# Scan inputs of an S5 layer: full-width matmuls with two turned copies, or half-width matmuls with one

## The chip, the cores and the metric

One core of one Trainium2 chip runs the whole program; the other cores are idle. The metric is device microseconds of one execution. PE is TensorE's matmul side and PEld its weight loads; DVE is VectorE, ACT ScalarE, POOL GpSimd, SP the queue that issues most transfers. Every fp32 matmul shows as two records in the trace, and so does its weight load.

## The reference, cut to what matters

Two encoder layers over 512 tokens of width 1024. Layer 0 mixes tokens with a bidirectional diagonal state-space scan, layer 1 with a short convolution; each is followed by cross-attention into 256 memory tokens and a squared-ReLU MLP. The change is in the scan of layer 0:

```python
u = (h @ w_in).reshape(bsz, seq, SSM_GROUPS, SSM_GROUP)
for r in range(N_DIR):
    a_bar = jnp.exp(lam * dt)
    b_bar = ((a_bar - 1.0) / lam)[..., None] * b
    bu = jnp.einsum('gph,lbgh->lbgp', b_bar, u_c)
    if r == 1:
        bu = jnp.flip(bu, axis=0)
    _, states = lax.associative_scan(_ssm_combine, (a_seq, bu), axis=0)
    if r == 1:
        states = jnp.flip(states, axis=0)
    y = y + jnp.einsum('ghp,lbgp->blgh', c, states).real
```

There are 64 groups of 16 channels, 64 complex states in each group, and two directions.

## The kernel before

The scan is done in chunks of T = 8 tokens, NC = 64 chunks. Partitions 0 to 63 hold the 64 states of the forward direction, partitions 64 to 127 those of the reverse direction. What a chunk adds to the state at its end (the scan input of the chunk) is a matmul over the chunk's 8 x 16 input values; 63 sequential scan steps then run over the chunks for all 64 groups and both directions at once.

The steps around the change, each named as in the code:

- `win_mm`, `u_evac` (lines 688 to 702): the in-projection on PE, scaled by DVE, stored to DRAM and loaded again as `U[i]`, with (channel, token in chunk) on the partitions and the 64 chunks along the free side.
- `sf_gen`, `sf_transpose` (lines 494 to 519): for each block `b` of 8 groups DVE makes the coefficients `sfT` with five operations (`sf_step(b)`, which also has ACT's `bb` copies), PE transposes them with `tr` banks and ACT copies them to `sf`.
- `s_mats` (lines 523 to 531): for real and imaginary part (`ri`), eight matmuls, one for each group, fill one PSUM bank `ps_s`; ACT copies the bank into `estate`, whose free layout is (chunk, part, group). The forward half, partitions 0 to 63, is copied as it is, the reverse half with the chunks turned round, since the reverse direction starts with the last chunk.
- `q_tables`, `q_ops` (lines 452 to 457 and 535 to 538): DVE makes the output coefficients `Q`, four blocks before the scan and four between its first steps.
- `scan_ops`, `scan_run` (lines 594 to 603 and 775 to 784): the 63 steps, four dependent operations on DVE each, in place in `estate`. The first one reads chunk 0 of `estate` for all groups.
- `strips`, `y_intra`, `kvp` (lines 543 to 584 and 711 to 713): beside the scan PE computes impulse responses (`w` banks), which go through DRAM and come back as `mt`, the in-chunk part of the output, and, as filler, the keys and values of the memory (`kv0_gen`, lines 629 to 656), whose weight blocks ACT's queue loads (`kv_load`).
- `p_early`, `p_copy`, `y_carry` (lines 674 to 683 and 586 to 592): the states are copied out as carried-in states, half of them when 42 steps are done, and multiplied with `Q`.

This whole phase stands under a manual schedule: each engine runs its instructions in the order of the code, so the calls of lines 721 to 865 are the order. Small tiles of 4 KB a partition come from one pool of 30 pages, which `sf`, `sfT`, `gt` and `Q` share: a tile waits until the last reader of the page's earlier tile is done. PSUM has a pool of six banks for `tr`, `ps_s`, `w`, `u` and `y`.

Of the kernel before, what the change touches and what calls it, by code (L numbers as in the profile page):

```python
# [46 lines left out]
def tile_encoder(ctx, tc, xT, xN, memT, memN, small, b_re, b_im, c_re, c_im, a_w_in, a_w_glu,  # L47
# [31 lines left out]

    # ------------------------------------------------------------------ constants  # L80
    sm = cpool.tile([P, NSM], F32, name="sm")
# [14 lines left out]

    # ------------------------------------------------------------------ weight stream
    def wblock(w, c0, k0=0):
# [71 lines left out]
    def lin_block(xs, hooks=None):  # L170
        """One 256-column block: two psum banks, accumulated over the 8 k-tiles."""
        t = next_block()
        ps = [bank([S], "lin") for _ in range(2)]
        for k in range(KT):
            if hooks and k in hooks:
                for f in hooks[k]:
                    f()
            xh, xl = xs(k)
            for m in range(2):
                mm3(ps[m], wsl(t, k, m, 0), wsl(t, k, m, 1), xh, xl, k == 0, k == KT - 1)  # L180
        return ps

    class Act2:
        """hi/lo split activation: 8 k-tiles, two per page."""

# [27 lines left out]

    # ------------------------------------------------------------------ norm helpers
    class Stats:
# [30 lines left out]

    # ================================================================== S5 phase
    man = ExitStack()
# [29 lines left out]
    def token_rstd(srcs, dst):  # L278
        """rows of tokens -> 1/rms of every token, on all partitions of dst."""
        n = len(srcs)  # L280
        ss = s5pool.tile([P, n], F32, name=nm("ss"))
        for i in range(n):
            act.activation(srcs[i], srcs[i], AF.Square, accum_out=ss[:, i:i + 1])
        act.activation(ss, ss, AF.Sqrt, scale=1.0 / D, bias=epsb)

        def rest():
            v.reciprocal(ss, ss)
            dg = page([n, P], F32, "dg")
            for i in range(n):
                act.activation(dg[:, i, :], ident, AF.Copy, scale=ss[:, i:i + 1])  # L290
            ps = fbank([n, P], "rb")
            pe.matmul(ps, lhsT=ones, rhs=dg, start=True, stop=True)
            act.copy(dst, ps.rearrange("p n q -> p (n q)"))
        return rest

    # ---- discretisation tables, [(r,p), g]
    def sm64(o):
# [29 lines left out]
    def exp_ops(o, x):  # L327
        """o = exp(x): x = n ln2 + r, polynomial in r, exponent bits from n."""
        xc, n, r, acc = t64(), t64(), t64(), t64()
        ni = t64().bitcast(I32)  # L330
        cs = [1.0 / math.factorial(k) for k in range(9)]
        ops = [lambda: ts(xc, x, 88.5, ALU.min, -87.0, ALU.max),
               lambda: ts(n, xc, 1.0 / math.log(2.0), ALU.mult, MAGIC, ALU.add),
               lambda: ts(n, n, -MAGIC, ALU.add),
               lambda: stt(r, n, -0.693359375, xc, ALU.mult, ALU.add),
               lambda: stt(r, n, 2.12194440e-4, r, ALU.mult, ALU.add),
               lambda: ts(n, n, 127.0, ALU.add, float(2**23), ALU.mult),
               lambda: ts(acc, r, cs[8], ALU.mult),
               lambda: v.tensor_copy(ni, n)]
        for k in range(7, 0, -1):  # L340
            ops.append(lambda k=k: stt(acc, acc, cs[k], r, ALU.add, ALU.mult))
        ops.append(lambda: stt(o, acc, 1.0, ni.bitcast(F32), ALU.add, ALU.mult))
        return ops

    def merge(*lists):
        """Round-robin over independent chains."""
        lists = [list(x) for x in lists]
        while any(lists):
            for x in lists:
                if x:  # L350
                    x.pop(0)()
# [40 lines left out]
    def cmul_ops(dst, a, b, n, u):  # L392
        """dst[n,G] = a[n,G] * b[G] (complex)."""
        br, bi = bc(b[0], n), bc(b[1], n)
        return [lambda: tt(dst[0], a[0], br, ALU.mult), lambda: tt(u[0], a[1], bi, ALU.mult),
                lambda: tt(dst[1], a[0], bi, ALU.mult), lambda: tt(u[1], a[1], br, ALU.mult),
                lambda: tt(dst[0], dst[0], u[0], ALU.subtract), lambda: tt(dst[1], dst[1], u[1], ALU.add)]
# [25 lines left out]

    # per-token coefficient tables, [(r,p), g, 8]; the reverse direction runs the other way
    es = page([2, G, 8], F32, "es")
# [32 lines left out]

    # ---- helpers of the scan pipeline
    bb = s5pool.tile([P, 2, 65 * 16], F32, name="bb")  # L460
# [3 lines left out]
    def gen_ops(b, X, xs, E, E2, flip, name):  # L464
        """8 groups of the complex products X * E, three products each; flip: the second
        operand carries -Im X and the imaginary part comes out negated."""
        g0 = 8 * b
        shape = [8, 8, 16] if flip else [8, 16, 8]
        r0, r1 = [page(shape, F32, name) for _ in range(2)]
        u = page(shape, F32, "gt")  # L470

        def bx(a):
            return a[:, g0:g0 + 8, :].unsqueeze(2 if flip else 3).to_broadcast([P] + shape)

        def be(a):
            return a[:, g0:g0 + 8, :].unsqueeze(3 if flip else 2).to_broadcast([P] + shape)

        M, A, B = ALU.mult, ALU.add, ALU.subtract
        d, s_ = be(E2[0]), be(E2[1])
        ops = [(u, bx(xs), be(E[:, 0]), M), (r0, bx(X[1]), d if flip else s_, M),  # L480
               (r1, bx(X[0]), s_ if flip else d, M)]
        if flip:
            ops += [(r0, u, r0, A), (r1, u, r1, B)]
        else:
            ops += [(r0, u, r0, B), (r1, u, r1, A)]
        return [r0, r1], ops
# [36 lines left out]
    def s_mats(b):  # L523
        for ri in range(2):
            ps = bank([8, NC], "ps_s")
            for g in range(8):
                pe.matmul(ps[:, g, :], lhsT=sf[b][ri][:, g, :], rhs=U[b // 2][:, 8 * (b % 2) + g, :],  # L527
                          start=True, stop=True)
            o = estate[:, :, ri, 8 * b:8 * b + 8].rearrange("p s g -> p g s")
            act.copy(o[0:64], ps[0:64])  # L530
            act.copy(o[64:128, :, ::-1], ps[64:128])  # L531

# [10 lines left out]
    def strips(t16, fill):  # L543
        """impulse responses of 16 groups -> banded chunk matrices M[(h,j), g, (t,h')]."""
        ps0, ps1 = bank([4, T, 16], "w0"), bank([4, T, 16], "w1")
# [32 lines left out]
    def y_intra(i):  # L578
        """in-chunk part of 16 groups, rows (8 groups' half, chunk)."""
        yps[i] = [(fbank if i == 3 else bank)([4, P], "y") for _ in range(2)]  # L580
# [23 lines left out]

    # ---- memory keys and values of layer 0, fp32 products
    mn = {}
# [22 lines left out]
    def kv0_gen(mp):  # L629
        """Yields after every matmul (all fp32, N = 256)."""  # L630
        for i in range(8):
# [28 lines left out]
    def p_part(b, s0, s1, engs):  # L660
        """states after steps s0..s1-1 as the carried-in states of the next chunk."""
        for ri in range(2):
# [21 lines left out]

    # ---- in-projection, fp32 products, with the scan inputs pipelined behind it
    ups = {}
# [88 lines left out]
    def scan_run(n, extra=()):  # L775
        """n scan steps; the ops of extra go into the gaps between dependent ones."""
        extra = list(extra)
# [32 lines left out]

    # ---- outputs: carried states through C a^k on top of the in-chunk part; gelu; to feature rows
    zf = []
# [71 lines left out]
    def norm_feed(k, st, a, vec):  # L884
        """h[k] is final for this sub-layer: statistics and the scaled hi/lo operand."""
        if a is not None:
# [3 lines left out]

    # ---- gated linear unit and out-projection
    z2 = Act2("z2")
# [23 lines left out]

    # ------------------------------------------------------------------ cross attention
    def kv_tiles():
# [89 lines left out]

    # ------------------------------------------------------------------ squared-relu MLP
    def mlp(hn_, st, vec, last):  # L1010
# [33 lines left out]
    def finish(md, r2, st):  # L1044
        """The last block, one half of the tokens after the other, each with its final norm."""
        t = next_block()
# [71 lines left out]

    # ------------------------------------------------------------------ layer 1: short conv
    cz = Act2("cz")  # L1120
# [42 lines left out]

    # ---- keys and values of layer 1
    kh, vh = kv_tiles()
# [30 lines left out]
def _layout(i):  # L1196
    """Layout only: transposes, broadcasts, padding and packing."""
    f = np.float32
# [41 lines left out]
```

## Time and profile before

| | us |
|---|---|
| three runs | 1489.86, 1492.65, 1494.39 |
| median | 1492.65 |
| span of the profiled execution | 1489.2 |
| PE busy | 1452.9 (98%) |
| DVE busy | 866.4 (58%) |
| ACT busy | 558.8 (38%) |

For the profiled execution the span alone is given, from its first instruction to its last; no device time of its own. A busy share is a mean over the whole span: the scan phase, the first 240 us, has other limits than the dense layers behind it, where PE does nearly nothing else but `lin` matmuls. What the change moves has to be read from the stretch from 60 to 215 us.

### The profile page before, as it was taken

How to read it: one execution, taken by the hardware profiler on the slowest of the kernel's cores; microseconds unless marked ns; L12 is line 12 of the kernel's file. 1: busy time of each engine (PE TensorE's matmuls, PEld its weight loads, DVE VectorE, ACT ScalarE, POOL GpSimd, SP SyncE). 2: the span in 40 equal slices, each digit the busy share in tenths (PEclk: the TensorE clock that was granted, in tenths of full speed). 3: DMA queues.
4: the chain of work that ended last, by engine and by line, in shares of the span. 5: the costliest groups of instructions: out<-in, count | busy, mean ns of one | idle time of the engine just before them, and what ended most of it. 6: DMA issues, size and time to landing. Idle time of an engine off the chain costs nothing.

```text
span 1489.2 us, 18984 instructions
## 1 busy us (share of the span) xinstructions
PE 1452.9 (98%) x7890; PEld 1200.7 (81%) x7890; DVE 866.4 (58%) x1377; ACT 558.8 (38%) x815; POOL 2.6 (0%) x25
## 2 busy tenths in 40 slices
PE   7998998999999999999999999999999999999997
PEld 3596777888888888888888888988888888888886
DVE  8877987466566444444358455546657444444435
ACT  4684166344344232231334233434445323132321
POOL 0000000000000000000000000000000000000000
PEclk9979999999999999999999999999999999999998
DMA  8613644322034323223214223622124332323201
GB/s 288 196 31 87 173 137 141 114 86 85 29 113 141 114 85 100 99 89 110 85 57 141 85 85 102 209 87 87 56 85 141 89 109 85 114 85 102 96 1 57
DMA packets 157302, 155.46 MB, mean 104 GB/s; under 512 B 11424, under 2 KB 152864, under 8 KB 157216
## 3 DMA queue, kind: packets, MB, share of 16 engines
q1 hardware_dynamic: 149888, 146.91, 31.3%
q10 hardware_dynamic: 7328, 7.34, 1.6%
q8 instruction: 62, 1.02, 0.3%
q14 instruction: 24, 0.20, 0.0%
HBM read 148.08 MB, written 6.16 MB: 104 GB/s over the span
## 4 chain that ended last, share of the span: by engine, by line
PE 90%; DVE 5%; ACT 3%; DMA 1%; issue 0%; SPq 0%; DVEq 0%; ACTq 0%
PE lin L168 25%; PE lin L166 25%; PE lin L167 25%; PE u L692 4%; PE ps_s L527 2%; DVE estate L312 1%; DVE sc L312 1%; DVE Q L312 1%; PE kv L167 1%; PE kv L168 1%; PE kv L166 1%; ACT pt L666 1%; PE tr L516 1%; ACT estate L531 1%; ACT estate L530 1%; PE sc L168 1%
## 5 line engine op out<-in xcount | busy, mean ns | idle before, releaser
L144 DVE TENSOR_TENSOR wl<-st,wh 128x1024 fp32r<-128x1024 f32 x224 | 270.7, 1222 | 171.5 <-ACT wh L143 170.8
L143 ACT CAST wh<-st 128x1024 fp32r<-128x1024 f32 x224 | 231.6, 1050 | 320.9 <-PE lin L167 293.1
L166 PE MATMUL lin<-hnh,wh 128*128 128x512 f32 x832 | 326.4, 392 | 0.0
L168 PE MATMUL lin<-hnh,wl 128*128 128x512 f32 x832 | 324.1, 390 | 0.0
L167 PE MATMUL lin<-hnl,wh 128*128 128x512 f32 x832 | 324.0, 389 | 0.0
L166 PE MATMUL lin<-mid,wh 128*128 128x512 f32 (+1 forms) x528 | 202.7, 384 | 0.0
L167 PE MATMUL lin<-mid,wh 128*128 128x512 f32 (+1 forms) x528 | 202.2, 383 | 0.0
L168 PE MATMUL lin<-mid,wl 128*128 128x512 f32 (+1 forms) x528 | 202.2, 383 | 0.0
L167 PEld LDWEIGHTS lin<-hnl,wh 128*128 128x128 f32 x832 | 156.2, 188 | 33.3 <-issue 1.2
L166 PEld LDWEIGHTS lin<-hnh,wh 128*128 128x128 f32 x832 | 156.2, 188 | 33.3 <-issue 1.2
L168 PEld LDWEIGHTS lin<-hnh,wl 128*128 128x128 f32 x832 | 156.2, 188 | 32.5
L166 PEld LDWEIGHTS lin<-mid,wh 128*128 128x128 f32 x528 | 99.3, 188 | 19.5
L167 PEld LDWEIGHTS lin<-mid,wh 128*128 128x128 f32 x528 | 99.3, 188 | 19.3
L168 PEld LDWEIGHTS lin<-mid,wl 128*128 128x128 f32 x528 | 99.2, 188 | 19.3
L312 DVE TENSOR_TENSOR relu<-relu,lin 128x512 f32<-128x512 f32 x64 | 43.7, 684 | 104.5 <-ACT relu L1024 104.5
L312 DVE TENSOR_TENSOR mo<-lin,r 128x512 f32<-128x512 f32 (+1 forms) x66 | 44.3, 675 | 102.0 <-PE lin L168 101.8
L1024 ACT ACTIVATE relu<-lin 128x512 f32<-128x512 f32 x64 | 38.1, 596 | 128.2 <-PE lin L168 127.8
L887 ACT ACTIVATE hnh<-h,sm 128x512 fp32r<-128x512 f32 x40 | 28.7, 718 | 132.0 <-DVE h L312 118.8
L692 PE MATMUL u<-xbig,st 128*128 128x512 f32 x128 | 57.6, 610 | 8.0 <-DMA st<-in_a_w_in_dram 8.0
L312 DVE TENSOR_TENSOR h<-lin,h 128x512 f32<-128x512 f32 x32 | 21.8, 692 | 67.3 <-PE lin L168 57.8
L692 PEld LDWEIGHTS u<-xbig,st 128*128 128x128 f32 x128 | 24.9, 196 | 38.4 <-issue 37.5
L1026 ACT CAST mid<-relu 128x512 fp32r<-128x512 f32 x64 | 39.5, 617 | 42.4 <-DVE relu L312 41.7
(215 smaller groups left out, 2004.0 us busy)
## 6 DMA issues: line engine op xcount, KB each, us to landing
st<-in_f_w_dram SPq DMA_DIRECT2D x64, 1024.0 KB, 5.5
st<-in_b_w_in_dram SPq DMA_DIRECT2D x12, 1024.0 KB, 5.3
st<-in_x_w_kv_dram SPq DMA_DIRECT2D x10, 1024.0 KB, 5.4
st<-in_x_w_q_dram SPq DMA_DIRECT2D x8, 1024.0 KB, 5.2
st<-in_x_w_o_dram SPq DMA_DIRECT2D x8, 1024.0 KB, 5.1
st<-in_x_w_kv_dram ACTq DMA_DIRECT2D x6, 1024.0 KB, 7.2
mt<-wd SPq DMA_DIRECT2D x32, 128.0 KB, 4.3
st<-in_a_w_glu_dram SPq DMA_DIRECT2D x4, 1024.0 KB, 5.5
```

The source lines that it names most:

```text
L143: act.copy(hi, src)
L144: v.tensor_tensor(out=lo, in0=src, in1=hi, op=ALU.subtract)
L166: pe.matmul(ps, lhsT=wh, rhs=xh, start=start, stop=False)
L167: pe.matmul(ps, lhsT=wh, rhs=xl, start=False, stop=False)
L168: pe.matmul(ps, lhsT=wl, rhs=xh, start=False, stop=stop)
L312: v.tensor_tensor(out=o, in0=a, in1=b, op=op)
L516: pe.transpose(ps[:, i, :], sfT[b][ri][:, g].rearrange("p h j -> p (h j)"), ident)
L527: pe.matmul(ps[:, g, :], lhsT=sf[b][ri][:, g, :], rhs=U[b // 2][:, 8 * (b % 2) + g, :], start=True, stop=True)
L692: pe.matmul(ups[i, m], lhsT=win[i][:, k, m * P:(m + 1) * P], rhs=hn[k // 2][:, k % 2, :], start=(k == 0), stop=(k == KT - 1))
L887: act.activation(a.hi(k), hk(k), AF.Copy, scale=gain(vec, k))
L1024: act.activation(r_, ps[m], AF.Relu)
L1026: act.copy(md[:, k, 0, :], r_)
```

## The change

`s_mats` is rewritten. Each group's matmul becomes two, one for each direction: the weight slice is the 64 columns of that direction, and the output goes to its half of the partitions. For the reverse direction the moving operand `u` is read with the chunks backwards, so the bank holds that half already turned round. The bank is laid out as (chunk, group) instead of (group, chunk), so a matmul writes its 64 chunks with a step of 8 elements. One copy of all 128 partitions then moves the bank into `estate`: it reads the bank straight through and writes runs of 8 elements. The rest of the diff takes out comments and docstrings.

```diff
     def s_mats(b):
         for ri in range(2):
-            ps = bank([8, NC], "ps_s")
+            ps = bank([NC, 8], "ps_s")
             for g in range(8):
-                pe.matmul(ps[:, g, :], lhsT=sf[b][ri][:, g, :], rhs=U[b // 2][:, 8 * (b % 2) + g, :],
-                          start=True, stop=True)
-            o = estate[:, :, ri, 8 * b:8 * b + 8].rearrange("p s g -> p g s")
-            act.copy(o[0:64], ps[0:64])
-            act.copy(o[64:128, :, ::-1], ps[64:128])
+                u = U[b // 2][:, 8 * (b % 2) + g, :]
+                for r in range(2):
+                    rs = slice(64 * r, 64 * r + 64)
+                    pe.matmul(ps[rs, :, g], lhsT=sf[b][ri][:, g, rs], rhs=u[:, ::-1] if r else u,
+                              start=True, stop=True)
+            act.copy(estate[:, :, ri, 8 * b:8 * b + 8], ps)
```

On PE, before, the last bank of `s_mats(1)` and the first transposes of block 4 (`tr`), which follow it:

```order
L527 MATMUL ps_s_607<-U_350,sf_402 128x64 [waits Activation_49]
L527 MATMUL ps_s_607<-U_350,sf_402 128x64 x7
L516 MATMUL tr_646<-sm,sfT_480 128x128 [waits DVE_49]
L516 MATMUL tr_646<-sm,sfT_480 128x128 x3
L516 MATMUL tr_652<-sm,sfT_480 128x128 [waits PE_49,Activation_49]
```

The same place of the changed kernel:

```order
L530 MATMUL ps_s_628<-U_350,sf_402 64x64 [waits Activation_49]
L530 MATMUL ps_s_628<-U_350,sf_402 64x64 x15
L516 MATMUL tr_674<-sm,sfT_480 128x128 [waits DVE_49,Activation_49]
L516 MATMUL tr_674<-sm,sfT_480 128x128 x3
L516 MATMUL tr_680<-sm,sfT_480 128x128 [waits DVE_49]
```

Eight matmuls of a bank became sixteen of half the width, nothing changed places, and the transposes' banks are other ones, with other waits.

On ACT, before, the copies of the last two blocks' banks (`s_mats(6)`, `s_mats(7)`), and the first copy of the strips:

```order
L530 COPY estate<-ps_s_849 64x8x64 [waits PE_49]
L531 COPY estate<-ps_s_849 64x8x64
L530 COPY estate<-ps_s_860 64x8x64 [waits PE_49]
L531 COPY estate<-ps_s_860 64x8x64
L530 COPY estate<-ps_s_871 64x8x64 [waits PE_49]
L531 COPY estate<-ps_s_871 64x8x64
L530 COPY estate<-ps_s_882 64x8x64 [waits PE_49]
L531 COPY estate<-ps_s_882 64x8x64
L567 COPY wt_1178<-w_278_1055 128x4x128 [waits PE_49,Activation_49]
```

The same place of the changed kernel:

```order
L532 COPY estate<-ps_s_933 128x64x8 [waits PE_49]
L532 COPY estate<-ps_s_951 128x64x8 [waits PE_49]
L532 COPY estate<-ps_s_969 128x64x8 [waits PE_49]
L532 COPY estate<-ps_s_987 128x64x8 [waits PE_49]
L568 COPY wt_1290<-w_278_1167 128x4x128 [waits PE_49,Activation_49]
```

Two copies of 64 partitions for each bank became one of 128, and nothing else moved.

On DVE, before, `sf_step(7)`, the last coefficients of the scan inputs:

```order
L312 TENSOR_TENSOR gt_717<-bs_239,es_230 128x1024 [waits PE_49]
L312 TENSOR_TENSOR sfT_715<-bf_102,es_13_231 128x1024 [waits PE_49]
L312 TENSOR_TENSOR sfT_716<-bf_101,es_13_231 128x1024 [waits PE_49,Activation_49]
L312 TENSOR_TENSOR sfT_715<-gt_717,sfT_715 128x1024 [waits DVE_49]
L312 TENSOR_TENSOR sfT_716<-gt_717,sfT_716 128x1024 [waits DVE_49]
```

The same place of the changed kernel:

```order
L312 TENSOR_TENSOR gt_773<-bs_239,es_230 128x1024 [waits PE_49]
L312 TENSOR_TENSOR sfT_771<-bf_102,es_13_231 128x1024 [waits PE_49]
L312 TENSOR_TENSOR sfT_772<-bf_101,es_13_231 128x1024 [waits DMAHW0_49]
L312 TENSOR_TENSOR sfT_771<-gt_773,sfT_771 128x1024 [waits DVE_49]
L312 TENSOR_TENSOR sfT_772<-gt_773,sfT_772 128x1024 [waits DVE_49]
```

The order on DVE is the same; the third operation has a page that a transfer frees, where it had one that PE and ACT free.

## Rows read from the trace of the kernel before

**Rows 1.** The chain that ended last, 60 to 240 us: start us, us, engine, what
```profile
75.08 12.60 PE ps_s L527 x64
...
87.67 3.05 PE tr L516 x16
...
98.72 1.06 ACT estate L530
...
126.49 1.06 ACT estate L531
...
213.70 0.58 ACT V L653
```

**Rows 2.** DVE's timeline, 60 to 215 us: start us, us, [idle before <-releaser]
```profile
84.30 1.23 DVE L312 TENSOR_TENSOR gt<-bs,es 128x1024 f32<-128x1024 f32 x1 [5.42 <-PE ps_s L527]
...
87.71 1.23 DVE L312 TENSOR_TENSOR sfT<-bf,es 128x1024 f32<-128x1024 f32 x1 [2.19 <-PE ps_s L527]
...
89.49 1.22 DVE L312 TENSOR_TENSOR sfT<-bf,es 128x1024 f32<-128x1024 f32 x1 [0.55 <-PE tr L516]
...
127.58 0.49 DVE L312 TENSOR_TENSOR sc<-estate,a 128x128 f32<-128x128 f32 x2 [8.72 <-ACT estate L531]
...
213.69 0.61 DVE L312 TENSOR_TENSOR estate<-estate,sc 128x128 f32<-128x128 f32 x2
```

**Rows 3.** Groups by shape, 60 to 130 us: count | busy us, mean ns | idle before
```profile
L530 ACT COPY estate<-ps_s 64x512 f32<-64x512 f32 x16 | 16.7, 1046 | 5.2 <-PE ps_s L527 5.0
...
L531 ACT COPY estate<-ps_s 64x512 f32<-64x512 f32 x16 | 16.7, 1045 | 0.2
...
L517 ACT COPY sf<-tr 128x512 f32<-128x512 f32 x24 | 12.3, 600 | 5.4 <-PE tr L516 5.3
```

**Rows 4.** ACT's timeline, columns as in rows 2
```profile
89.80 1.06 ACT L754 ACTIVATE cf<-cf 128x1024 f32<-128x1024 f32 x1
...
191.10 0.79 ACT L664 COPY pt<-estate 64x336 f32<-64x336 f32 x1 [1.02 <-DVE estate L312]
...
200.64 0.38 ACTq L103 DMA_DIRECT2D st<-in_x_w_kv_dram  x1
```

**Rows 5.** Windows: us, busy PE PEld DVE ACT POOL, granted clock, DMA share, GB/s
```profile
75.00:87.50 12.50, 12.42 (x65) 12.43 (x66) 5.11 (x5) 7.67 (x10) 0.00 (x0) 0.56 0.27 74
...
78.00:90.00 12.00, 12.00 (x58) 12.00 (x58) 3.85 (x4) 7.90 (x9) 0.00 (x0) 0.50 0.19 42
...
90.00:92.00 2.00, 2.00 (x20) 2.00 (x18) 2.00 (x3) 1.98 (x4) 0.00 (x0) 0.95 0.00 0
```

**Rows 6.** Weight loads of L527 and L590: ns min/median/max, first and last start
```profile
L527 PEld LDWEIGHTS ps_s<-U,sf x256: 186/193/338, 75.1 to 122.4; 128*128 128x128 f32 x128
...
L590 PEld LDWEIGHTS y<-Q,pt x256: 132/137/138, 215.3 to 235.8; 128*64 128x64 f32 x128
```

**Rows 7.** Timelines of PE and of its weight loads (PEld), columns as in rows 2
```profile
90.45 7.22 PEld L527 LDWEIGHTS ps_s<-U,sf 128*128 128x128 f32 x64
...
97.54 1.79 PEld L516 LDWEIGHTS tr<-sm,sfT 128*128 128x128 f32 x16
...
122.69 0.61 PE L553 MATMUL w<-Q,bb 64*32 64x112 f32 x32
...
123.24 0.32 PE L560 MATMUL w<-cf,bb 128*32 128x16 f32 x16
...
123.39 0.23 PE L563 MATMUL w<-dd,sm 128*32 128x16 f32 x8
...
187.46 8.90 PE L640 MATMUL kv<-st,mem 128*128 128x256 f32 x40
...
206.52 7.15 PE L640 MATMUL kv<-st,mem 128*128 128x256 f32 x32 [2.22 <-DMA st<-in_x_w_kv_dram]
...
224.77 3.47 PEld L590 LDWEIGHTS y<-Q,pt 128*64 128x64 f32 x64 [0.17 <-issue]
```

**Rows 8.** DVE's copies out of estate at L664, columns as in rows 6
```profile
L664 DVE COPY pt<-estate x16: 290/444/600, 214.2 to 221.7; 64x168 f32<-64x168 f32 x8, 64x504 f32<-64x504 f32 x8
```

## The prediction, made before the changed kernel ran

> **What bounds the kernel now.** I began with the chain of waits that ended last, then took the DVE, ACT and PE timelines around the place of the change, then the granted clock by stretch.
>
> Most of the span is dense linear layers, which the change does not touch; it sits in `s_mats`, between 75 and 128 us. There the chain [rows 1] runs over PE's `ps_s` matmuls from 75.08, passes to ACT at 98.72, and stays with ACT's copies out of PSUM until 126.49 + 1.06 = 127.55. DVE shows what that costs [rows 2]: it stands idle for 8.72 us, from 118.86 to 127.58, before the first step of the scan, because that step reads `estate` columns which the last of these copies writes.
>
> What follows is two chains that run side by side and end together. DVE does the 63 scan steps, one after the other, from 127.58 to 213.69 + 0.61 = 214.30. PE does the strips, the in-chunk products and the key/value matmuls from 122.69 on [rows 7], right behind the last `ps_s`, and ACT's last V copy behind them ends at 213.70 + 0.58 = 214.28 [rows 1]. The carried-in states are then copied by ACT, so the stage after 214.3 waits for both. The gain is therefore the smaller of two shifts: X, by which the scan starts earlier, and Y, by which PE reaches the strips earlier.
>
> **Baseline.** The profiled execution has a span of 1489.2 us; its own device time is not listed. The three runs gave 1489.86 to 1494.39, median 1492.65, which is 3.45 above the span. I take the lead-in and the tail as unchanged and subtract the gain from the median.
>
> **ACT's part.** Today 32 copies of 64x512, 16 at 1046 ns and 16 at 1045 [rows 3], 33.5 us. Each element lands 512 bytes from the one before. After: 16 copies of 128x512 whose output comes in runs of eight adjacent elements. No row has that pattern. The cheap end is a contiguous copy of the same shape, 600 ns [rows 3]; the dear end is today's 1046 ns. That is 9.6 to 16.7 us, a saving of 17 to 24 us of ACT time. I take no value between, because it will not matter: from 89.80 [rows 4] to 127.55 ACT is busy without a gap, 37.75 us, of which 24 copies (25.1 us) are these; the other 12.7 us stay. With 12 copies in their place it needs 20 to 25 us behind the fourth bank's copy, so ACT would be done between 102 and 107 us. That is earlier than DVE, below.
>
> **PE's part.** 128 fp32 matmuls of 128x64 become 256 of 64x64, each shown as two records, so 256 records become 512. Today's record takes 111 ns at full clock (64 between 90.45 and 97.54 [rows 7]). That is the weight load: its rows last 193 ns for 128 columns and 137 for 64 [rows 6], so 0.87 ns a column and 111 ns for 128. For 64 columns it is 56 ns. The moving side costs as much an element: 40 records of 256 elements in 8.90 us [rows 7], 0.87 ns each, so 56 ns for 64. A new record needs 56 ns of load and 56 of streaming in its own half of the array; what matters is whether the two halves overlap. `y_carry` has the same weight shape, also alternates between halves, and streams 128 elements (111 ns) per record, yet does 64 records in 3.47 us, 54 ns each [rows 7]: streaming overlaps. Loads: the 16 records of L560, 32 columns each (28 ns by the same rate), start 123.24 and are through by 123.39 [rows 7], 9 ns each: loads overlap too. So **28 ns a record**, 14.3 us for all 512 against 28.4 us today.
>
> The change also reads the chunks backwards on the moving side and writes PSUM with a step of eight elements. No row of PE shows either. The nearest rows: ACT backwards (L531) costs the same as forwards (L530) [rows 3], factor 1.0. For the step, ACT's 1046 ns for 64x512 against 600 ns contiguous is 1.74; DVE's copies out of `estate`, with a 512-byte step on the reading side, take 290 ns for 168 elements and 600 for 504 [rows 8], 0.92 ns an element, DVE's usual rate, factor 1.0. PE streams at 0.87 ns an element, closest to DVE's pace, so I take 1.0; the far end is 1.74 or, rounded up, 56 ns a record, and a dearer price is a rival below.
>
> Switching between 64-wide and 128-wide matmuls, some dozen times: the strips change shape before and behind L560, and its 16 records are through in 0.15 us all the same [rows 7], so I put at most 0.1 us on each, 1.2 us on PE. The cover is Y minus X, 6.5 us below; without it, 1.2 us.
>
> **The sum.** `s_mats(0)` starts at 75.08 as now: its waits are unchanged. The clock stands at 0.56 of full over the 75 to 87.5 us and 0.95 from 90 to 92 [rows 5], which is 1.5 us at 2.4 GHz, to 76.5, and 1.2 GHz behind that until about 90. The first 128 records then take 1.42 us (51 records) and 77 x 56 ns = 4.3 us: done at 80.8 instead of 87.7.
>
> DVE: `sf_step(7)` waits on pages that `s_mats(1)` frees [rows 2], 5.42 us with the third quarter of these records, 2.19 with the last, and 0.55 for a transpose. The third quarter ends at 79.0, when DVE is only just free (78.88), the last at 80.8; the third wait now names a transfer, which I take to be the store of `ut` before it, and landed. So the operation that starts at 89.49 today starts one operation of 1.14 us behind 80.85, at 82.0: 7.5 us earlier. Everything up to the fourth Q block follows without a gap, so the scan can start at 118.86 - 7.5 = 111.3. **X = 127.58 - 111.3 = 16.2 us.**
>
> PE: transposes of block 4 at half clock, 3.05 us [rows 1], to 83.9; then, at full clock, 384 records x 28 ns = 10.75 us and three groups of transposes of 1.79 [rows 7]: 100.0. In general, with r us a record, 82.1 + 640 r. **Y = 122.69 - 100.0 = 22.7 us.** The last `estate` copy follows within a microsecond, or by ACT's own sum by 107: both ahead of 111.3, so DVE sets X. The strips need the second Q block, 7.5 us earlier than today, at 100: in time.
>
> The PE chain ends with one transfer: ACT issues the last key/value block at 200.64 behind its early state copies, which wait for the scan (1.02 us at 191.10) [rows 4], and PE starts on it at 206.52 [rows 7]. So it shifts with X: 184.4, 190.3, V copied 198.1, and the scan ends at 214.3 - 16.2 = 198.1 too. Behind that nothing changes: **1492.65 - 16.2 = 1476.4 us.**
>
> **Rivals.**
> - *The halves give nothing on PE* (loads serialise, or the stepped write costs a factor 2): 56 ns a record. For it: the y rows fit serial loads as well as parallel streaming; against it: L560. PE ends at 82.1 + 35.8 = 117.9, Y = 4.8; DVE keeps its page waits, X = 8.7. Gain 4.8: 1487.9.
> - *The stepped PSUM write or backward read is dear*, as much as today's whole load: 111 ns for each of 512 records. PE ends at 153.1, 30.4 us late, and takes strips and scan with it: 1523. It decides from 63 ns a record on, where 82.1 + 640 r passes 122.69. For it: no row shows such an access on PE, and ACT pays 1.74 for a step; against it: backwards is free on ACT and a step is free on DVE. The Trainium skill, in Advanced Engine Details and Errata under Memory Cachelines, says that any non-contiguous pattern in PSUM slows matmuls significantly. It gives no factor, and no run here shows it yet.
> - *The clock stays low.* The lighter matmuls might not bring it back at 84 as I assume; it stayed at 1.2 GHz through 12 us of fully busy `ps_s` today [rows 5]. If to 90, X is about 13; if throughout, PE ends at 83.9 + 21.5 + 9.2 = 114.6, Y = 8 and the early state copies wait for the PE chain, gain about 9. 1480 to 1484. Against it: `y_carry` at 54 ns ran at full clock.
> - *The gain goes elsewhere*: a page or a transfer behind 128 us becomes late and eats all but 4 us, 1489 to 1496. I find no row for it; PE's slack of 6 us would have to vanish as well.
>
> **How the numbers follow.** Main case 0.60 (1476.4), clock 0.12 (1482), no gain on PE 0.14 (1487.9), dear access 0.07 (1523), gain gone 0.07. About 0.3%, 4.5 us, is what can be told from no change. Main and clock cases are faster beyond it; the no-PE-gain case, 4.8, falls half on either side: faster 0.79, same 0.14, slower 0.07. Range: with none of the DVE waits X is 16.9, 1475.8, and the runs reach 2.8 below their median: 1473. Upwards it takes in the no-PE-gain case: 1488.
>
> **What would show it.** Right: `ps_s` records near 28 ns at full clock in pairs, PE at the strips near 100, DVE without idle time before the scan or less than 1 us, the scan starting near 111, ACT done before. Wrong: `ps_s` records of 56 ns or more, DVE still waiting for `estate`, a half-speed clock beyond 90 us, or the V copy after the end of the scan.

## The result: 1474.25 us, and the profile after

The changed kernel takes 1474.25 us, median of 4 runs (1473.18 to 1475.26). The kernel before, run beside it, took 1491.26 (1489.22 to 1494.39), so the ratio is 0.988 with a 95% interval of 0.9864 to 0.9896: 17.0 us faster. The forecast was 1476.4, within 1473 to 1488. Of the 2.2 us between forecast and result, 1.4 lie in the base: I subtracted from 1492.65, and the runs beside the changed kernel had 1491.26. The gain itself was 17.0 where I had 16.2.

The profiled execution took 1473.65 us, with a span of 1471.9, against a span of 1489.2 before. Lines below `s_mats` have moved by one (L527 is now L530, the copy is L532).

PE first. This is its timeline over the changed stage, with the columns of [rows 2]:

```profile
74.14 3.95 PE L530 MATMUL ps_s<-U,sf 128*64 128x64 f32 x128 [1.45 <-ACT sf L517]
78.02 1.97 PE L516 MATMUL tr<-sm,sfT 128*128 128x128 f32 x16
79.91 4.27 PE L530 MATMUL ps_s<-U,sf 128*64 128x64 f32 x128
...
93.88 3.95 PE L530 MATMUL ps_s<-U,sf 128*64 128x64 f32 x128
97.76 0.61 PE L554 MATMUL w<-Q,bb 64*32 64x112 f32 x32
```

The stage begins at 74.14, 0.94 us earlier than in the trace of before; that lead is older than the change, and it has to come off every shift below. 128 records take 3.88 us (74.14 to 78.02), 30.3 ns each with the step to the transposes, where 64 full-width ones took 12.60 [rows 1]. PE reaches the strips at 97.76, before at 122.69 [rows 7]: Y is 24.0 us without the lead.

The windows show a second thing (columns as in [rows 5]; first the changed kernel, then the kernel before):

```profile
74.00:84.00 10.00, 9.77 (x272) 9.40 (x272) 10.00 (x11) 8.99 (x19) 0.00 (x0) 1.00 0.36 97
84.00:98.00 14.00, 14.00 (x331) 13.15 (x334) 13.91 (x14) 12.91 (x28) 0.00 (x0) 1.00 0.02 4
98.00:116.00 18.00, 16.89 (x488) 11.95 (x470) 18.00 (x26) 3.08 (x6) 0.00 (x0) 1.00 0.37 94
```

```profile
74.00:84.00 10.00, 8.92 (x48) 8.93 (x49) 4.88 (x5) 6.62 (x9) 0.00 (x0) 0.63 0.45 131
84.00:98.00 14.00, 14.00 (x102) 14.00 (x102) 10.56 (x11) 12.17 (x17) 0.00 (x0) 0.78 0.01 2
98.00:116.00 18.00, 16.55 (x119) 16.17 (x118) 18.00 (x17) 17.73 (x24) 0.00 (x0) 0.81 0.00 0
```

The granted clock is 1.00 throughout, where it had been 0.63, 0.78 and 0.81. DVE, the third number of the busy times, is now busy for 10.00 of 10 us and 18.00 of 18. Its timeline says the same in single rows:

```profile
77.86 1.22 DVE L312 TENSOR_TENSOR gt<-bs,es 128x1024 f32<-128x1024 f32 x1
78.99 2.35 DVE L312 TENSOR_TENSOR sfT<-bf,es 128x1024 f32<-128x1024 f32 x2
...
109.10 0.49 DVE L312 TENSOR_TENSOR sc<-estate,a 128x128 f32<-128x128 f32 x2
...
195.18 0.61 DVE L312 TENSOR_TENSOR estate<-estate,sc 128x128 f32<-128x128 f32 x2
```

The first three rows are the operations that waited in [rows 2]: 5.42 us, 2.19 and 0.55 (the two of the second row), and 8.72. None of them has a bracket any more. The scan starts at 109.10, before at 127.58: 18.5 us earlier, 17.5 without the lead of 0.94. That is X. The last row is the last scan step.

ACT's group of copies (columns as in [rows 3]) has 16 members in place of 32, at 632 ns each. It still waits for PE, 1.9 us in place of 5.2, and PE's matmuls no longer wait for it, as they did for 1.31 us before:

```profile
L532 ACT COPY estate<-ps_s 128x512 f32<-128x512 f32 x16 | 9.2, 632 | 1.9 <-PE ps_s L530 1.9
```

The end of the stage, ACT's timeline and then PE's, answers to the last lines of [rows 1], [rows 4] and [rows 7]:

```profile
172.60 0.78 ACT L665 COPY pt<-estate 64x336 f32<-64x336 f32 x1 [9.05 <-DVE estate L312]
...
182.11 0.37 ACTq L103 DMA_DIRECT2D st<-in_x_w_kv_dram  x1
...
197.14 0.58 ACT L654 COPY V<-kv 128x512 f32<-128x512 f32 x1 [10.88 <-PE kv L641]
197.75 1.67 ACT L667 COPY pt<-estate 64x168 f32<-64x168 f32 x4
```

```profile
170.81 7.14 PE L641 MATMUL kv<-st,mem 128*128 128x256 f32 x32 [0.97 <-DMA st<-in_x_w_kv_dram]
187.48 9.62 PE L641 MATMUL kv<-st,mem 128*128 128x256 f32 x32 [9.53 <-DMA st<-in_x_w_kv_dram]
```

The scan ends at 195.18 + 0.61 = 195.79, but the last V copy at 197.72, and the state copies follow it at 197.75. Before, both chains ended within 0.02 us of each other. They no longer do: the last block of 32 records took 9.62 us and not 7.14, behind 9.53 us in which PE had nothing to do. The clock was low in that block, as a window over its first part shows (columns as in [rows 5]):

```profile
184.00:194.00 10.00, 6.52 (x19) 5.38 (x20) 9.35 (x39) 2.22 (x4) 0.00 (x0) 0.57 0.29 98
```

So the end of the stage moved by 214.28 - 197.72 = 16.6 us, 15.6 without the lead; the span moved by 17.3. At the first `lin` matmul the shift is still 16.6 us (238.13 before, 221.56 here), so the other 0.7 us come from the dense layers. The stage itself accounts for 15.6 us of the measured 17.0 in this pair of traces; the rest I cannot put down to the change.

### The profile page after: what moved, and what is told of

It is laid out like the page before. It is cut to its first block, busy times and chain, and to the rows that moved or that the text cites. A ratio compares the mean times of both kernels' runs of the same rounds, so it can differ in the third digit from the quotient of the medians.

```text
span 1471.9 us, 19469 instructions
## 1 busy us (share of the span) xinstructions
PE 1432.1 (97%) x8146; PEld 1178.2 (80%) x8146; DVE 865.9 (59%) x1377; ACT 534.0 (36%) x799; POOL 4.9 (0%) x25
## 4 chain that ended last, share of the span: by engine, by line
PE 92%; DVE 4%; ACT 2%; DMA 1%; issue 0%; SPq 0%; ACTq 0%; DVEq 0%
PE lin L166 26%; PE lin L168 26%; PE lin L167 26%; PE u L693 4%; DVE estate L312 1%; DVE sc L312 1%; PE kv L168 1%; PE kv L167 1%; PE kv L166 1%; ACT pt L667 1%; PE ps_s L530 1%; PE tr L516 1%; PE kv L641 1%; PE kv L639 1%; DMA wd<-wt 1%; DVE Q L312 1%
## 5 line engine op out<-in xcount | busy, mean ns | idle before, releaser
L693 PEld LDWEIGHTS u<-xbig,st 128*128 128x128 f32 x128 | 25.1, 198 | 37.2 <-issue 30.3
```

The source lines that it names most:

```text
L693: pe.matmul(ups[i, m], lhsT=win[i][:, k, m * P:(m + 1) * P], rhs=hn[k // 2][:, k % 2, :], start=(k == 0), stop=(k == KT - 1))
```

## Experiments

All ratios are to the kernel before in the same set of runs, with 95% intervals; the diffs are against the changed kernel, and `...` stands for what is left out of a line. Line numbers differ by a few from kernel to kernel.

### Each half of the change alone

**One copy, full-width matmuls.**

```
-                for r in range(2):
-                    rs = slice(64 * r, 64 * r + 64)
-                    pe.matmul(ps[rs, :, g], lhsT=sf[b][ri][:, g, rs], ...)
+                pe.matmul(ps[:, :, g], lhsT=sf[b][ri][:, g, :], ...)
```

> The copy's half of the change alone: full-width matmuls as before (128 of 128x64), bank laid out chunk outermost, one full-height copy for each bank. Left out: the reverse half's chunks are not turned round, so the reverse direction is computed on unturned inputs. My theory (both halves of the change are needed, PE then limits): the records stay at 111 ns at full clock, because they are bound by 128 columns of weights; PE reaches the strips near 117, DVE starts the scan near 119, gain 4 to 6 us of the 17. Rival 1 (ACT's copies were the whole limit): gain 15 to 17 us. Rival 2 (the stepped write into PSUM is dear where a matmul is full width): records above 125 ns and a gain under 3 us.

Measured: 1483.28 us, ratio 0.9948 (0.9933 to 0.9963), 8.6 us gained. Half of the full change, then, more than the 4 to 6 us that I expected, and more than the 4.8 us of my first rival, which has the same matmul time and the same single copy. PE's and DVE's timelines:

```profile
74.91 12.94 PE L527 MATMUL ps_s<-U,sf 128*128 128x64 f32 x64 [1.45 <-ACT sf L517]
...
90.38 7.26 PE L527 MATMUL ps_s<-U,sf 128*128 128x64 f32 x64
...
116.96 0.61 PE L551 MATMUL w<-Q,bb 64*32 64x112 f32 x32
...
198.66 7.14 PE L638 MATMUL kv<-st,mem 128*128 128x256 f32 x32 [0.51 <-DMA st<-in_x_w_kv_dram]
```

```profile
84.48 1.23 DVE L312 TENSOR_TENSOR gt<-bs,es 128x1024 f32<-128x1024 f32 x1 [5.76 <-PE ps_s L527]
...
118.65 0.49 DVE L312 TENSOR_TENSOR sc<-estate,a 128x128 f32<-128x128 f32 x2
```

DVE keeps its waits for PE (5.76 here) and loses only the last one, for `estate`: X = 127.58 - 118.65 = 8.9, or 8.8 without the lead of 0.17 that this trace has, as I had worked out (8.7). PE reaches the strips at 116.96, so Y = 5.6 by the same reckoning. If the gain were the smaller of X and Y, it would be 5.6. It is more, because PE had slack behind the strips: the last block stood 2.22 us waiting for its load before [rows 7] and stands 0.51 here, which makes 1.7 us, and some 0.4 us more were made up on the way there. The last V copy ended 7.8 us earlier, at 206.44, 1.1 us behind the scan's end.

**Half-width matmuls, two copies.**

```
-            ps = bank([NC, 8], "ps_s")
+            ps = bank([8, NC], "ps_s")
...
-                    pe.matmul(ps[rs, :, g], ..., rhs=u[:, ::-1] if r else u,
+                    pe.matmul(ps[rs, g, :], ..., rhs=u, ...)
...
-            act.copy(estate[:, :, ri, 8 * b:8 * b + 8], ps)
+            o = estate[:, :, ri, 8 * b:8 * b + 8].rearrange("p s g -> p g s")
+            act.copy(o[0:64], ps[0:64])
+            act.copy(o[64:128, :, ::-1], ps[64:128])
```

> The matmuls' half of the change alone: 256 half-width matmuls in pairs, but the bank stays group outermost, nothing is read backwards, and two half-height copies turn the reverse half round as before. My theory: ACT limits; from 74 us on it has 33.5 us of estate copies and 15 us of other copies, so the scan starts between 122 and 124, gain 3 to 6 us. Rival (the matmuls were the whole limit): gain 15 to 17 us, scan near 110.

Measured: 1488.68 us, ratio 0.9981 (0.9972 to 0.9991), 3.2 us gained. The groups and DVE's timeline say why:

```profile
L533 ACT COPY estate<-ps_s 64x512 f32<-64x512 f32 x16 | 16.7, 1046 | 0.2
```

```profile
L530 PE MATMUL ps_s<-U,sf 128*64 128x64 f32 x512 | 20.4, 247 | 10.3 <-ACT estate L533 7.5 <-ACT sf L517 2.8
```

```profile
123.45 0.49 DVE L312 TENSOR_TENSOR sc<-estate,a 128x128 f32<-128x128 f32 x2 [9.68 <-ACT estate L533]
```

The matmuls are fast and PE waits 10.3 us for ACT in between; ACT, with 32 copies of about 1050 ns as before, is still the last to finish, and DVE waits 9.68 us for it. The scan starts 4.1 us earlier, 4.7 counted from the start of the stage. Less than that is gained, and the trace shows the last V copy ending at 212.84, 2.7 us behind the scan: the last key/value block comes late, behind 4.17 us of idle time on PE, and takes 9.96 us. The two halves alone gain 8.6 + 3.2 = 11.8 us, together 17.0: with one of them done, the other engine is what ends last. The Trainium skill warns of the second case (TensorEngine Tiling (Array Packing), PSUM Bottleneck): tiling speeds up TensorE but not the copies out of PSUM. This trace agrees, with PE's 10.3 us of waiting for ACT's copies.

### The access patterns on PE

**Contiguous bank, the step on ACT's writing side.**

```
-            ps = bank([NC, 8], "ps_s")
+            ps = bank([8, NC], "ps_s")
...
-                    pe.matmul(ps[rs, :, g], ...
+                    pe.matmul(ps[rs, g, :], ...
...
-            act.copy(estate[:, :, ri, 8 * b:8 * b + 8], ps)
+            act.copy(estate[:, :, ri, 8 * b:8 * b + 8].rearrange("p s g -> p g s"), ps)
```

> The whole change, except that the bank stays group outermost: the matmuls write PSUM in one straight run of 64, and the one full-height copy does the step, each element 512 bytes from the one before. Expected: the copy takes about 1.05 us instead of 0.63, 16.8 us in all, ACT ends near 105, still ahead of DVE at 109; the time stays within 1.5 us of the changed kernel, 17 us under the kernel before. If the stepped write into PSUM costs what the records show above 28 ns (30.5 measured), they come down to 28 here. Rival (ACT's copies set the start of the scan in the changed kernel as well): the scan starts some 7 us later, gain 10 us.

Measured: 1476.87 us, ratio 0.9902 (0.9887 to 0.9917). PE's first records, and ACT's copies:

```profile
74.14 3.95 PE L530 MATMUL ps_s<-U,sf 128*64 128x64 f32 x128 [1.44 <-ACT sf L517]
```

```profile
L532 ACT COPY estate<-ps_s 128x512 f32<-128x512 f32 x16 | 15.9, 1185 | 0.0
```

128 records take 3.95 us with a contiguous PSUM row and 3.95 with the step of eight elements: the stepped write costs TensorE nothing. What the chunk-outermost bank buys is ACT's side, 632 ns a copy instead of 1185, and that is worth little here, since ACT had time: the scan starts at 109.11, as in the changed kernel, and the last V copy ends at 198.68, 1.0 us later. By the medians the loss is 2.6 us, more than the 1.5 that I allowed, but the intervals overlap.

**Forward read.**

```
-                    pe.matmul(..., rhs=u[:, ::-1] if r else u,
+                    pe.matmul(..., rhs=u,
```

> The changed kernel with one edit: the reverse half's matmuls read the chunks forwards as the forward half's do, so that nothing on the moving side of TensorE runs backwards. Left out is the turning of the reverse half's chunks. Theory (the backward read costs nothing, as its mirror on ACT cost nothing): records stay at 30.5 ns, all but the few tenths they lie above the 28 of the prediction, and the time is that of the changed kernel within 1.5 us. Rival (the backward read is what lifts 28 to 30.5 ns): records of 28 ns or fewer, PE at the strips 1.3 us earlier, and still no change of the end, since PE has slack there.

Measured: 1473.96 us, ratio 0.9884 (0.9866 to 0.9903).

```profile
75.13 3.95 PE L530 MATMUL ps_s<-U,sf 128*64 128x64 f32 x128 [1.46 <-ACT sf L517]
```

3.95 us again. The backward read is free, and it is not what lifts the record from 28 to 30 ns.

**The halves one after the other**: all forward matmuls of a bank, then all reverse ones.

```
-            for g in range(8):
-                u = ...
-                for r in range(2):
+            for r in range(2):
+                for g in range(8):
+                    u = ...
```

> The whole change with the eight forward matmuls of a bank first and the eight reverse ones behind them, so neighbours share a half of the array. My theory (the gain on PE is that neighbours in different halves load and stream side by side): 54 to 58 ns a record instead of 30.5, PE some 13 us later at the strips (near 111 if the clock stays at 2.4 GHz, near 118 if it falls as in the kernel before), the scan 3 to 10 us later than in the changed kernel, gain 7 to 14 us. Rival (half-width weights alone are the gain, the order does not matter): 30 ns a record, gain 17 us.

Measured: 1475.8 us, ratio 0.99 (0.9883 to 0.9917), about 16 us gained.

```profile
75.11 6.42 PE L530 MATMUL ps_s<-U,sf 128*64 128x64 f32 x128 [1.45 <-ACT sf L517]
...
108.44 0.61 PE L554 MATMUL w<-Q,bb 64*32 64x112 f32 x32
...
180.52 7.14 PE L641 MATMUL kv<-st,mem 128*128 128x256 f32 x32 [0.20 <-DMA st<-in_x_w_kv_dram]
190.03 7.14 PE L641 MATMUL kv<-st,mem 128*128 128x256 f32 x32 [2.37 <-DMA st<-in_x_w_kv_dram]
```

Records of 50 ns (6.35 us for 128) instead of 30: work in the two halves of the array overlaps when it alternates, and mostly does not when it comes in blocks of one half. PE reaches the strips 9.7 us later than in the changed kernel (10.7 less the later start of this stage, 0.97), and the time is nearly the same. I had expected a gain of 7 to 14 us. That was too little: DVE waits only 1.4 us for PE in all, the scan starts 1.5 us later counted from the start of the stage, and PE has slack for the rest. The late PE also gives something back: the last block waits only 2.37 us and keeps its clock (7.14 us), and the last V copy ends at 197.81, 0.5 us ahead of the scan (198.30).

### What ends the stage now

The next four ran on one chip, the changed kernel among them.

> The changed kernel once more, on the chip of the two edits that follow, so that differences of 2 to 5 us can be read. Expected: ratio near 0.988 to the kernel before, scan end near 195.8, last V copy ended near 197.7, one PE idle time of about 9.5 us ahead of the last key/value block and half clock in it.

Measured: 1474.61 us, ratio 0.9887 (0.9872 to 0.9903). The scan ends at 196.22 and the last V copy at 197.59. PE stood idle 12.04 us before its last block, more than the 9.5 expected, and the block took 9.15.

**The last load from SP's queue.**

```
-        kvst[i] = stage_load(..., None if i < 2 else act)
+        kvst[i] = stage_load(..., None if i < 2 or i == 7 else act)
```

> The changed kernel with one edit: the load of the last key/value block is issued from SP's queue, no longer from ACT's behind the early state copies. Theory 1 (the last block, late and at half clock, is what ends the stage in the changed kernel, so it has eaten 1.9 us of the scan's shift): PE runs the last block right behind the one ahead of it, near 178 to 185 us, the last V copy is done long before the scan, the state copies start at the scan's end near 195.8 instead of 197.75, and the time is up to 1.9 us below the changed kernel's. Rival: PE then stands idle some 10 us ahead of the carried-state matmuls, the clock falls there instead, these matmuls run at half speed on the path, and nothing is gained (within 1 us) or 1 to 2 us are lost.

Measured: 1473.0 us, ratio 0.9876 (0.9859 to 0.9892), 1.6 us below the changed kernel by the medians and not to be told from nothing. The load did go out early, at 173.85, and PE still waited:

```profile
187.09 8.97 PE L641 MATMUL kv<-st,mem 128*128 128x256 f32 x32 [5.20 <-ACT V L654]
...
197.79 7.62 PE L591 MATMUL y<-Q,pt 128*64 128x128 f32 x128
```

The theory named the wrong holder. The PSUM bank for block 7 is that of block 5, and block 5's V copy stands behind the 16 early state copies in ACT's order, as the load does. Even so the last V copy now ends at 196.69, 0.4 us ahead of the scan (197.05), and counted from the start of the stage the state copies begin 1.7 us earlier than in the changed kernel of this set.

**The tables on POOL**, four operations of DVE ahead of the Q blocks:

```
     def q_tables():
+        pt = lambda o, a, b, op: nc.gpsimd.tensor_tensor(out=o, in0=a, in1=b, op=op)
-        tt(dd, ...); tt(eq2[0], ...); tt(eq2[1], ...); tt(cf[2], ...)
+        pt(dd, ...); pt(eq2[0], ...); pt(eq2[1], ...); pt(cf[2], ...)
```

> The changed kernel with one edit: the four table operations behind the seventh sf_step (1.22 + 2 x 0.69 + 0.42, 3.0 us of DVE in all) are done by POOL, which is idle there and has their inputs early. Theory 1 (in the changed kernel DVE alone sets the start of the scan): the scan starts 2.9 to 3.0 us earlier, near 106.1, with still no wait for estate or for PE, the early state copies, the last load and the end of the stage shift with it, and the time falls by 2.5 to 3 us. Rival 1 (PE or ACT stands right behind DVE): DVE shows a wait for PE or ACT ahead of the scan and gains less than 1.5 us. Rival 2: operations of POOL lengthen those of DVE beside them, so that DVE's 1.22 us operations of that stretch grow and the scan starts less than 2 us earlier.

Measured: 1475.42 us, ratio 0.9889 (0.9875 to 0.9904): nothing, 0.8 us above the changed kernel by the medians, within the noise. POOL's and DVE's timelines:

```profile
82.06 5.96 POOL L453 TENSOR_TENSOR cs<-cf,cf 128x1024 f32<-128x1024 f32 x1 [31.34 <-ACT cf L756]
```

```profile
88.05 1.22 DVE L312 TENSOR_TENSOR gt<-cs,eq 128x1024 f32<-128x1024 f32 x1 [2.26 <-POOL cs L453]
```

The fourth operation waits for ACT's negated table, takes 5.96 us on POOL where DVE needs 1.22, and DVE waits 2.26 us for it. None of the three theories had named that: POOL itself stands behind DVE. The two edits together:

> The changed kernel with both edits, the last key/value load on SP's queue and the four table operations on POOL. Theory 1 (scan and last block are the two chains that end the stage, and their shifts add up): scan end near 192.9, state copies right behind it, 4 to 5 us below the changed kernel. Rival (idle PE, half clock in the carried-state matmuls): 2 to 3 us below the changed kernel, as with the tables alone.

Measured: 1471.45 us, ratio 0.9864 (0.9849 to 0.9878). DVE still waits 2.26 us for POOL and PE's last block 8.77 us for block 5's V copy, but that block starts at 185.86, where the changed kernel of this set has it at 187.83. That is 2.0 of the 3.2 us between their medians; the rest I can't account for. The 4 to 5 us of theory 1 did not come, since the tables on POOL hardly move the scan: it ends at 195.81 and not near 192.9.

**Early state copies behind the V copies of blocks 5 and 6.**

```
-    kvp(16)
+    kvp(48)
     for b in range(4):
         p_early(b)
-    kvp(48)
+    kvp(16)
```

> The changed kernel with one edit: the early state copies stand behind the V copies of key/value blocks 5 and 6 in ACT's order, no longer ahead of both, so that neither the last load nor the last block's PSUM bank waits for them. Theory 1 (in the changed kernel the last block, held up by ACT's order, ends the stage, 1.9 us behind the scan): the last load is issued near 170 and not at 182, PE's last block runs near 178 to 185 us without a long wait before it, the early copies run from 178 to 191, the last V copy behind them near 192, and the state copies start at the scan's end near 196; the time falls by 1.5 to 2 us. Rival: with the last block done early PE stands idle for 10 us or more before the carried-state matmuls, the clock falls there instead of in the last block, these records go from 54 to about 108 ns, and the time is that of the changed kernel or 1 to 2 us more.

Measured: 1471.71 us (1471.63 to 1472.07), ratio 0.9868 (0.9849 to 0.9887). The ratios' intervals overlap with the changed kernel's, but all four runs lie below the lowest of its eight (1473.18), and below the lowest of the kernel with the forward read, which ran on the same chip (1472.93). PE, then ACT, then windows around the place:

```profile
173.02 14.05 PE L641 MATMUL kv<-st,mem 128*128 128x256 f32 x64 [0.93 <-DMA st<-in_x_w_kv_dram]
...
194.00 1.98 PE L584 MATMUL y<-mt,U 128*64 128x128 f32 x16 [5.91 <-ACT V L654]
196.59 8.43 PE L591 MATMUL y<-Q,pt 128*64 128x128 f32 x128 [0.61 <-ACT pt L667]
```

```profile
193.37 0.59 ACT L654 COPY V<-kv 128x512 f32<-128x512 f32 x1
195.22 1.63 ACT L667 COPY pt<-estate 64x168 f32<-64x168 f32 x4 [1.26 <-DVE estate L312]
```

```profile
194.00:200.00 6.00, 5.39 (x58) 4.88 (x60) 5.80 (x21) 4.74 (x11) 0.00 (x0) 0.60 0.00 0
```

Blocks 6 and 7 run together in 14.05 us, at full clock, and the last V copy is done at 193.96. The state copies now wait for the scan and start at 195.22, 2.5 us earlier than in the changed kernel, although the stage began 0.4 us later. So the late last V copy, and the block ahead of it, did end the stage there. The rival is right in part as well: PE is idle for 5.91 us, the clock is at 0.60 in the window behind, and the first 128 carried-state records take 8.43 us, against 7.62 with the load on SP's queue, where the last block ran just before. These records cost 0.8 us of what was won.

**The same, with three of the tables on POOL**, all but the one that waits for ACT:

```
-        tt(dd, ...); tt(eq2[0], ...); tt(eq2[1], ...)
+        pt(dd, ...); pt(eq2[0], ...); pt(eq2[1], ...)
         tt(cf[2], ...)
```

> The edit of the kernel before this one, and in addition three of the four table operations (0.42 + 2 x 0.69, 1.7 us of DVE in all, whose inputs are ready long before) done by POOL; the fourth, which reads a table that ACT negates late, stays on DVE. Theory 1 (DVE alone sets the scan's start, and the scan alone the end): the scan starts 1.6 to 1.7 us earlier than in the kernel with the first edit alone, near 107.5, and the time falls by the same 1.5 to 1.7 us. Rival 1: POOL's operations stretch DVE's beside them or end so late that DVE waits, as with all four (2.26 us of waiting): 0 to 0.5 us. Rival 2: the chain over the last key/value block does not move with the scan and ends the stage: 0.

Measured: 1470.13 us (1469.62 to 1471.11), ratio 0.9857 (0.9841 to 0.9874), 1.6 us below the kernel with the first edit alone, and every run below its lowest. DVE's timeline:

```profile
84.63 1.22 DVE L312 TENSOR_TENSOR cs<-cf,cf 128x1024 f32<-128x1024 f32 x1
...
108.66 0.49 DVE L312 TENSOR_TENSOR sc<-estate,a 128x128 f32<-128x128 f32 x2
```

The stage began 0.68 us later than in the kernel with the first edit alone (75.24 against 74.56), and the scan still starts 0.87 us earlier (108.66 against 109.53): 1.55 us in all, for 1.7 us of DVE work taken away. DVE alone sets the start of the scan. That the scan alone sets the end is not shown: the last V copy ends at 195.26 here, 0.1 us ahead of the scan (195.38), and the state copies right behind it begin only 0.6 us earlier, counted from the start of the stage. How the rest of the 1.6 us comes about I did not trace. This version beats both kernels, the changed one by some 4 us and the one before by 21.

## Why the prediction held, point by point

- **What bounds the stage.** Right for its start: the scan on DVE, held up by `estate`, was the path, and after the change DVE sets its start without a wait. The last experiment shows it by taking work from DVE.
- **ACT.** Right: 632 ns a copy, near the cheap end of 600 to 1046. That no value had to be chosen is shown by the contiguous bank, where the copies took 1185 ns, beyond my dear end, and the scan started at 109.11 all the same. ACT was done at 98.47, not 102 to 107: it needed 19.7 us behind the fourth bank's copy, near the 20 of my cheap end, and that copy came early, at 78.72.
- **PE's record.** 28 ns was 30.3: the load of one half overlaps the other's, as I had read from L560, and serial loads, 56 ns a record or 7.2 us for 128, are refuted by the 3.95 us. The factor of 1.0 for the stepped write and the backward read held, each with its own run. On the stepped write, the rule that I had set against the change (the Trainium skill, Advanced Engine Details and Errata, Memory Cachelines: non-contiguous patterns in PSUM slow matmuls significantly) does not agree with these runs: 3.95 us for 128 records with the step and without. With it falls the rival of 1523 us.
- **The clock.** Wrong in the good direction. I let it fall at 76.5 and took 5.7 us for the first 128 records; it did not fall, and they took 3.9. In the traces it stood at 0.63 and 0.60 from 74 to 84 us in the two kernels with full-width matmuls, and at 1.00 in all with half-width ones, even where PE was busy for only 6.80 of the 10 us (half-width, two copies). The width alone does not decide it: later the same two-copy kernel ran at 0.57 from 84 to 92 us, and the one-copy kernel ran full-width matmuls at 1.00 from 98 to 116. What does I cannot say from these runs. With the clock up, DVE lost the second wait altogether, of which I had left 0.7 us, and X became 17.5, not 16.2: the four waits of [rows 2] make 16.9, a fifth of 0.4 us, for PE ahead of a Q block, I had not counted, and the last 0.2 come from operations that now follow each other without a gap.
- **The smaller of X and Y.** This step was loose. Y was not what I set against X: behind the strips PE has the slack of its wait for the last load, whose issue hangs on the scan. In the run with one copy the stage ended 7.8 us earlier where Y was 5.6, and the run with the halves apart lost 9.7 us of Y for next to nothing. That made the first rival too dear, a gain of 4.8 us (1487.9) where the run with its matmul time gained 8.6 (1483.28).
- **"Behind that nothing changes."** Wrong by 1.9 us, and the sum hid it. It is the last of the signs of being wrong that I had named: the V copy came after the end of the scan. The last load did move with the scan, from 200.64 to 182.11, but PE, now far ahead, had nothing to do for 9.53 us before it (2.22 before); the clock fell to 0.50, and the block took 2.5 us longer. Moving the copies that held it up gave 2.5 us back. So X was 1.3 us more than forecast and the end 1.9 us less than X, and these two misses nearly cancel: the stage ended 15.6 us earlier where I had 16.2. The rest of the 17.0 comes from outside the stage. The mechanism at the start of the scan was right; that the time came so close is in part luck.

## What to carry to other kernels

When two engines hand a stage back and forth, price the change of each alone as well as the pair: here they were worth 8.6 and 3.2 us alone and 17.0 together. A chain with slack must be given that slack before it is compared with another, and an engine that becomes much faster must be followed to its next idle time, since an idle TensorE may come back at half its clock. After the gain, look at the order of the instructions on the engine that serves both chains: one moved block of copies was worth another 2.5 us.

## What the runs showed of the hardware that I had not expected

- ACT writes runs of eight fp32 elements, 512 bytes apart, in 632 ns on average for 128x512 (592 with one copy and full-width matmuls, 595 with the halves apart); the same data element by element at that step takes 1185 ns. Short runs are enough. The Trainium skill (Advanced Engine Details and Errata, Memory Cachelines) says of SBUF that accesses run at full performance if the next ones hit the same 16-byte line, and that a different line for each access costs a penalty. The two runs agree: 632 ns with runs of eight, 1185 with single elements.
- Half-width matmuls take 30 ns a record when the halves alternate and 50 ns when each half's come in blocks; a full-width record, whose work two half-width ones do, takes 111 ns at full clock (one copy, 64 from 90.38 to 97.48).
- The clock stayed at 2.4 GHz in the changed kernel from 74 to 116 us, with half-width matmuls and transposes up to 97.76 and the strips behind them, where the first 64 full-width records of the same work took 12.60 and 12.94 us in two kernels, nearly all of it at 1.2 GHz. It is no rule for the width, as the figures under **The clock** above show.
- POOL needs 5.96 us for an fp32 addition of 128x1024 that DVE does in 1.22. Beside POOL's additions near 46 to 50 us, one operation of DVE took 2293 ns, where its like took 1212 (last experiment; 2292 and 2296 in the other two kernels with tables on POOL). In that place DVE had a wait behind it that covered it.
